# Longer rows and fewer transfers for the first stage's loads, with a new written order of that stage

## Chip, core and metric

The kernel runs on one core of a Trainium2 chip. The metric is the time of one execution on the device, in microseconds (us), median of three runs. Five engines work side by side: TensorE (PE, with its weight loads shown as PEld), VectorE (DVE), ScalarE (ACT), GpSimd (POOL) and SyncE (SP), which here only issues transfers. All transfers run on the core's 16 DMA engines.

## What is computed

One step of two transformer-like layers on 640 tokens (512 latent tokens and 128 prompt tokens) with 1024 channels. Cut to what the change touches, layer 0 begins so:

```
m     = silu(cond) @ w_mod[0] + b_mod[0]          # cond = c (latent) or c_ctx (prompt)
shift, scale = first two of the six 1024-wide parts of m
xm    = rmsnorm(x) * g * (1 + scale) + shift
q,k,v = split(xm @ w_qkv)                         # then attention, FFN, LRU layer, FFN
```

Everything is float32 in and out. Products that need precision are made of three products of rounded halves (hi*hi, hi*lo, lo*hi).

## The kernel before, in words

Activations lie transposed: channels on the 128 partitions in 8 blocks (index k), tokens along the row. The first stage, `start` (from line 339), makes shift and scale of the first sub-layer, the norm of x, the modulated x as two halves `hi` and `lo`, and the first eight blocks' sums of q and k of head pair 0. Behind it come attention (8 head pairs, up to about 350 us), the first FFN, the LRU layer and the second FFN, all of them chains of products on PE.

SP's queue of loads in the stage: the conditioning vectors (L1580), x in 8 transfers of one block each (L354, 320 KB, rows of 2560 bytes), then the adaLN weights `wm0` in 16 transfers of 512 KB with rows of 4 KB (`fetch`, L366): four groups g of two channel blocks, in each the scale part (j=1), then the shift part (j=0), each in two halves h of the contraction. Two weight tiles of q and k (L359) go behind the parts of group 0, two tiles of v behind all. SP issues a load when one of a few earlier ones has landed.

The stage's compute order on PE, DVE and ACT is written by hand in `START`, a list of steps that `in_order` chains on each engine. A letter is a step, the digits its arguments:

- `f`: a product of ones with 512 columns into a bank that nothing reads (L495), and `x`k n: the same with the first n columns of x block k (L492). Both only keep PE at work.
- `q`k, `a`k: square of x block k (ACT, L386) and its addition (DVE, L389). `m`: moments over the channels (PE, L394); `v j n`: variance, root and Newton step; `d`, `t`, `r`: diagonal matrix (DVE, L415), its spread over partitions (PE, L421), copy (ACT, L425).
- `p`g j h: a half piece of the adaLN product, 4 products of 256 columns (PE, L431; each has two instructions). `e`, `s`: copy and selection of a finished piece (ACT L436, PE L444). `A`k, `B`k: scale and shift of block k.
- `g`, `h`, `l`: x times scale and norm (DVE), its hi half (ACT), its lo half (DVE), for the latent (0) and prompt (1) tokens.
- `w`, `u`: hi and lo of a weight tile. `z`k part u: sums with block k, four products of 320 columns for part 0 (L481, L482) and two for part 1 (L479); `y`: the last eight (L488).

The order of work outside such lists is drawn up by a list scheduler at build time, from modelled times. The product that turns the conditioning vectors (L1582) stands ahead of the list in the program but is not in it; ScalarE's SiLU of them (L1583), the load of the table that holds the square root (L1585) and the copies that `p` needs hang on it. The first products of attention's v (L278) follow `y`.

Of the kernel before, what the change touches and what calls it, by code (L numbers as in the profile page):

```python
# [9 lines left out]
F32 = mybir.dt.float32  # L10
F32R = mybir.dt.float32r
AF = mybir.ActivationFunctionType
# [3 lines left out]
P = 128  # L16
D = 1024
KT = D // P
NLAT = 512
NTOK = 640  # L20
# [28 lines left out]
CHN = (3, 3, 4, 4, 4, 4)  # L49

START = (
# [6 lines left out]

TAIL = (
    "p0 T r0 p1 m r1 q0 q1 t1 p2 d r2 q2 t2 p3 x r3 s0 s1 q3 t3 p4 F0 r4 F2 s2 q4 t4 p5 r5 F4 s3 q5 t5 p6 r6 s4 F6 q6 s5 s6 p7 r7 q7 s7 y67 ")  # L60
# [6 lines left out]
def _lay(inp):  # L67
    g = {k: np.asarray(v) for k, v in inp.items()}

    def colmajor(v):  # L70
        return v.reshape(KT, P).T

    ng, cw = g["norm_g"], g["lru_conv_w"][0]
    vecs = [ng[0, 0], ng[0, 1], ng[1, 0], ng[1, 1], cw[0], cw[1], cw[2], cw[3], g["lru_conv_b"][0],
            g["lru_b_a"][0, 0], g["lru_b_a"][0, 1], g["lru_b_i"][0, 0], g["lru_b_i"][0, 1],
            g["lru_lam"][0, 0], g["lru_lam"][0, 1], g["state_h"][0, 0, 0], g["state_h"][0, 0, 1],
            g["b_mod"][0, :D], g["b_mod"][0, D:2 * D],
            g["final_g"], *(g["b_mod"][l, j * D:j * D + D] for l, j in MODS)]
    cols = np.concatenate([colmajor(v) for v in vecs], axis=1)

    rpb = g["attn_rpb"][0]

    def toeplitz(lo, hi, fill):
        e = np.full((NH, ROWS, 47, ROWS), fill, np.float32)
        for r in range(ROWS):
            e[:, r, lo + 23:hi + 24, :] = rpb[:, 7 - r:15 - r, lo + 15:hi + 16].transpose(0, 2, 1)
        return e

    inner = np.lib.stride_tricks.sliding_window_view(toeplitz(-15, 15, 0.0).reshape(NH, ROWS, 376), 256, axis=2)[:, :, 0:128:8]
    edge = np.stack([inner, inner], axis=1).transpose(0, 3, 2, 1, 4).reshape(NH, 16, ROWS, 2, 32, ROWS).copy()  # L90
    for i, c0 in enumerate((0, 48)):
        for cl in range(16):
            st = min(max(c0 + cl - 8, 0), 48)
            for j in range(32):
                if not st <= c0 - 8 + j < st + 16:
                    edge[:, 15 - cl, :, i, j] = NEG
    def tiles(w):
        return w.reshape(-1, P, w.shape[1] // P, P).transpose(2, 1, 0, 3)

    wq, gu, dn, wm = g["attn_w_qkv"][0], g["ffn_w_gu"], g["ffn_w_down"], g["w_mod"]  # L100
    arr = {
        "x": np.concatenate([np.roll(g["x_sample"].reshape(ROWS, 64, D).transpose(1, 0, 2), 8, axis=0).reshape(NLAT, D),
                             g["x_prompt"].reshape(P, D)]).T,
        "cc": np.stack([g["c"].reshape(KT, P), g["c_ctx"].reshape(KT, P)]).reshape(2 * KT, P),
        "ck": g["cache_k"].reshape(PAST, D).T,
        "cv": g["cache_v"].reshape(2, P, KT, P).transpose(2, 1, 0, 3),
        "wm0": wm[0, :, :2 * D].reshape(2, 4, P, 2, 4, 256).transpose(3, 4, 0, 2, 1, 5),
        "wm": wm.reshape(2, D, 6, D).transpose(0, 2, 3, 1).reshape(12, KT, P, D)[2:],
        "wqk": tiles(wq[:, :2 * D]),
        "wv": wq[:, 2 * D:].reshape(2, 4, P, 4, VW).transpose(3, 0, 2, 1, 4),  # L110
        "wo": tiles(g["attn_w_o"][0]),
        "wi": tiles(g["lru_w_in"][0]),
        "wg": np.stack([g["lru_w_a"][0], g["lru_w_i"][0]]).transpose(2, 3, 0, 1, 4),
        "wlo": tiles(g["lru_w_out"][0]),
        "gu": np.stack([tiles(w) for w in gu]),
        "dn": np.stack([tiles(w) for w in dn]),
        "cols": cols,
        "edge": edge.reshape(NH, P, 2, 256),
        "emid": toeplitz(-8, 7, NEG),
    }  # L120
    return {k: np.ascontiguousarray(v) for k, v in arr.items()}
# [13 lines left out]
def _pieces(t0, t1):  # L135
    return [(s, max(a, t0), min(b, t1)) for s, a, b in ((0, 0, NLAT), (1, NLAT, NTOK)) if max(a, t0) < min(b, t1)]


class _Step:
# [198 lines left out]
    def start(self, hi, lo, sp, big):  # L338
        nc, x = self.nc, self.x
# [9 lines left out]
        n = NB * P  # L349
        ssq = self.t([P, NTOK], F32, "ssq", 1, sp)  # L350
        rsb = self.t([P, NTOK], F32, "rsb", 1, sp)
        dg = self.t([P, NT, P], F32, "dg", 1, sp)
        for k in range(KT):
            nc.sync.dma_start(x[:, k], self.i["x"][k * P:k * P + P])  # L354
        raws = []

        def load(src):
# [3 lines left out]
        parts = {}  # L361

        def fetch(g, j):
            for h in range(2):
                w = self.t([P, 4, n], F32, f"sw{g}{j}{h}", 1, sp)
                nc.sync.dma_start(w, self.i["wm0"][j, g, h])  # L366
                parts[g, j, h] = w

        for g in range(KT // NB):
            for j in (1, 0):  # L370
                fetch(g, j)
                if g == 0:
                    load(self.i["wqk"][KT - j * KT])
# [7 lines left out]
        C, sq, pm, rows, pt, AB, z = _pieces(0, NTOK), [ssq], {}, {}, {}, {}, {}  # L381

        def square(k):
            if k:
                sq.append(idle[:, 2048 + k % 4 * NTOK:2688 + k % 4 * NTOK])
            nc.scalar.activation(sq[k], x[:, k], AF.Square)  # L386

        def add(k):
            nc.vector.tensor_tensor(ssq, ssq, sq[k], ALU.add)  # L389
# [104 lines left out]
        def fill():  # L494
            nc.tensor.matmul(acc[1][1], self.ones, self.ones.unsqueeze(1).broadcast_to([P, 4, P]), start=True, stop=True)  # L495

        steps = dict(f=fill, j=half, n=newton, q=square, a=add, m=moment, v=var, d=diag, t=spread, r=root, p=piece, e=row, s=select, A=scale, B=shift, g=gain, h=high, l=low,
                     w=weight, u=rest, z=sums, y=final, x=warm)
        with self.in_order():
# [367 lines left out]
    def heads_out(self, p, b0, pts, ppt, V, cv, op, O):  # L867
# [18 lines left out]
        for out, v, w, start, stop in parts():  # L886
            with self.tc.issue_after(first) if first is not None else nullcontext():
                mm = nc.tensor.matmul(out, v, w, start=start, stop=stop)  # L888
            first = first if first is not None else mm.ins
# [63 lines left out]
    def opening(self, w, hi, lo, gk, key, xd, l):  # L953
# [89 lines left out]
        with self.in_order():  # L1043
# [26 lines left out]
            f += 1  # L1070
            ps = mm(f, 1, range(KH))
            start(st)
            mm(f, 1, range(KH, KT), ps)
            gain(0, 0)
# [110 lines left out]
    def sum_weights(self, q, first=False):  # L1185
        for run, after in zip(self.s_sums(q), (self.pw, self.next)):
            with self.tc.issue_after(after):
                run(False)
        with self.tc.issue_after(self.last) if first else nullcontext():
            for i in range(2):  # L1190
                self.s_split(q, i)
# [355 lines left out]

    def load_x(self, src):
        for k in range(0, KT, 2):
            self.nc.sync.dma_start(self.x[:, k:k + 2], src[k * P:k * P + 2 * P].rearrange("(k p) t -> p k t", p=P))  # L1550

    def run(self):
        nc, tc, i, o = self.nc, self.tc, self.i, self.o
# [21 lines left out]
        with ExitStack() as banks:  # L1575
            self.pp = banks.enter_context(tc.tile_pool(name="psattn", bufs=1, space=bass.MemoryType.PSUM))
            self.begin(dict(tp=2, sp=2, op=1, quota=24))
            with tc.tile_pool(name="start", bufs=1) as sp:
                ccr = self.t([2 * KT, P], F32, "ccr", 1, sp)
                nc.sync.dma_start(ccr, i["cc"])  # L1580
                pc = self.ps("tp")
                nc.tensor.transpose(pc[:, :2 * KT], ccr, self.ident[:2 * KT, :2 * KT])  # L1582
                nc.scalar.activation(self.cs, pc[:, :2 * KT], AF.Silu)  # L1583
                nc.scalar.activation(ccr, ccr, AF.Silu)
                nc.scalar.activation(self.t([P, 1], F32, "dum", 1)[0:2 * KT], ccr[:, 0:1], AF.Sqrt, scale=0.0)  # L1585
                cd = dram.tile([2 * KT, P], F32, tag="cd", name="cd")
                nc.scalar.dma_start(cd, ccr)
                self.x = self.big(F32)
                acc, us = self.start(xhi, xlo, sp, wbig)
            self.mods = self.modulations()  # L1590

# [88 lines left out]
```

## Time and profile before

| | |
|---|---|
| median of 3 runs | 1486.8 us (1486.11 to 1486.82) |
| the profiled execution's own time | 1489.09 us |
| its span, first to last instruction | 1487.2 us |
| mean granted TensorE clock | 0.996 |
| PE busy | 1471.7 us (99%) |
| PEld / DVE / ACT busy | 97% / 73% / 49% |
| moved by DMA | 255.35 MB, mean 172 GB/s |

Busy PE time is modelled and overlaps; a PE that shows as busy can still wait between products. The granted clock is 1.00 at 2.4 GHz and 0.50 at 1.2 GHz. DMA share is the mean busy share of the 16 DMA engines: full stretches show 1.02 to 1.06.

### The profile page before, as it was taken

The numbers are of one execution on the slowest core, as the hardware profiler recorded it, in microseconds if no ns is written. First come the engines' busy times: TensorE is split into PE (matmuls) and PEld (weight loads), VectorE is DVE, ScalarE is ACT, GpSimd is POOL, SyncE is SP. The second block draws the span as 40 slices with busy tenths as digits, with TensorE's granted clock in tenths as the row PEclk, the third lists the DMA queues.
The fourth block names the chain that finished last, engine by engine and source line by source line (L and its number), as shares of the span: only waits on it lengthen the run. The fifth ranks groups of instructions, "written<-read, shape, count | busy, mean of one in ns | idle before, by whom it ended". The sixth has DMA issues, their size and how long they took to land.

```text
span 1487.2 us, 26374 instructions
## 1 busy us (share of the span) xinstructions
PE 1471.7 (99%) x10377; PEld 1439.8 (97%) x10377; DVE 1079.6 (73%) x2054; ACT 729.3 (49%) x1345; POOL 248.1 (17%) x325
## 2 busy tenths in 40 slices
PE   9999999999999999999999999999999999999997
PEld 5999999999999999999999999999999999999997
DVE  6788887876677788997876489985865665566555
ACT  5666766754333234323434298863644352434344
POOL 0001000000012222211210001112132322222311
PEclk9999999999999999999999999999999999999999
DMA  9545555443359899977863744267242231313122
GB/s 370 180 150 169 171 148 160 126 156 100 114 169 318 294 372 323 310 251 236 301 223 123 251 142 142 86 239 250 77 131 86 58 113 57 114 57 107 53 69 71
DMA packets 86026, 255.35 MB, mean 172 GB/s; under 512 B 9056, under 2 KB 22544, under 8 KB 85776
## 3 DMA queue, kind: packets, MB, share of 16 engines
q1 hardware_dynamic: 59152, 157.06, 32.4%
q0 software_dynamic: 26576, 96.49, 19.1%
q8 instruction: 81, 1.33, 0.4%
q14 instruction: 41, 0.34, 0.1%
q10 hardware_dynamic: 176, 0.13, 0.0%
HBM read 206.18 MB, written 43.53 MB: 168 GB/s over the span
## 4 chain that ended last, share of the span: by engine, by line
PE 89%; DVE 4%; DMA 3%; ACT 2%; issue 1%; POOL 1%; SPq 0%; DVEq 0%; ACTq 0%; POOLq 0%
PE mm L255 13%; PE mm L253 13%; PE mm L254 13%; PE mx L253 5%; PE mx L254 5%; PE mx L255 5%; PE mx L1203 3%; PE mx L1204 3%; PE mx L1205 3%; PE op L888 2%; PE gp L1412 2%; PE tp L806 2%; PE mc L1204 1%; PE mc L1203 1%; PE mc L1205 1%; PE mm L279 1%
## 5 line engine op out<-in xcount | busy, mean ns | idle before, releaser
L254 PE MATMUL mm<-big,whi 128*128 128x320 f32 (+3 forms) x1010 | 312.7, 310 | 0.3 <-DVE big L1530 0.3
L255 PE MATMUL mm<-big,wlo 128*128 128x320 f32 (+3 forms) x1010 | 312.2, 310 | 0.0
L253 PE MATMUL mm<-big,whi 128*128 128x320 f32 (+3 forms) x1010 | 310.9, 311 | 0.6 <-ACT big L1529 0.4
L292 DVE SCALAR_TENSOR_TENSOR mprod<-mraw,csb 128x1024 f32<-128x1024 f32 x160 | 195.0, 1218 | 18.2 <-DMA mraw<-in_wm 17.9
L254 PEld LDWEIGHTS mm<-big,whi 128*128 128x128 f32 x1010 | 190.5, 189 | 1.7 <-DVE big L1530 0.5
L253 PEld LDWEIGHTS mm<-big,whi 128*128 128x128 f32 x1010 | 189.6, 189 | 2.4 <-ACT big L1529 0.7
L255 PEld LDWEIGHTS mm<-big,wlo 128*128 128x128 f32 x1010 | 190.1, 189 | 1.0
L1529 ACT CAST whi<-raw 128x1024 fp32r<-128x1024 f32 (+2 forms) x103 | 105.4, 1025 | 150.9 <-PE mm L254 92.1
L1530 DVE TENSOR_TENSOR wlo<-raw,whi 128x1024 fp32r<-128x1024 f32 (+2 forms) x103 | 128.2, 1246 | 35.5 <-ACT whi L1529 35.3
L254 PE MATMUL mm<-big,whx 128*128 128x320 f32 (+3 forms) x443 | 137.4, 310 | 0.0
L255 PE MATMUL mm<-big,wlx 128*128 128x320 f32 (+3 forms) x443 | 137.3, 310 | 0.0
L253 PE MATMUL mm<-big,whx 128*128 128x320 f32 (+3 forms) x443 | 137.0, 310 | 0.0
L595 DVE SCALAR_TENSOR_TENSOR x<-mm,G,x 128x320 f32<-128x320 f32 (+3 forms) x202 | 81.4, 436 | 53.8 <-PE mm L255 48.5
L253 PE MATMUL mx<-big,whi 128*128 128x320 f32 (+3 forms) x318 | 99.3, 313 | 0.0
L254 PE MATMUL mx<-big,whi 128*128 128x320 f32 (+3 forms) x318 | 98.5, 310 | 0.1
L255 PE MATMUL mx<-big,wlo 128*128 128x320 f32 (+3 forms) x318 | 98.6, 310 | 0.0
L288 POOL DMA_DIRECT2D mraw<-in_wm x80 | 42.7, 534 | 311.5 <-DVE mprod L292 207.4
L254 PEld LDWEIGHTS mm<-big,whx 128*128 128x128 f32 x443 | 83.5, 189 | 0.0
L255 PEld LDWEIGHTS mm<-big,wlx 128*128 128x128 f32 x443 | 83.5, 189 | 0.0
L253 PEld LDWEIGHTS mm<-big,whx 128*128 128x128 f32 x443 | 83.4, 188 | 0.0
L1530 DVE TENSOR_TENSOR wlx<-sum,whx 128x1024 fp32r<-128x1024 f32 x40 | 51.0, 1274 | 35.1 <-ACT whx L1529 35.1
L255 PE MATMUL mx<-big,wlx 128*128 128x320 f32 (+3 forms) x229 | 70.9, 310 | 0.0
(396 smaller groups left out, 3854.4 us busy)
## 6 DMA issues: line engine op xcount, KB each, us to landing
raw<-in_gu SPq DMA_DIRECT2D x84, 512.0 KB, 3.7
mraw<-in_wm POOLq DMA_DIRECT2D x80, 512.0 KB, 5.4
raw<-in_dn SPq DMA_DIRECT2D x24, 512.0 KB, 3.6
sw<-in_wm SPq DMA_DIRECT2D x16, 512.0 KB, 10.1
raw<-in_wqk SPq DMA_DIRECT2D x16, 512.0 KB, 5.2
mraw<-in_wi POOLq DMA_DIRECT2D x16, 512.0 KB, 6.2
kwi<-kwh POOLq DMA_DIRECT2D x16, 512.0 KB, 6.0
kwi<-kwl POOLq DMA_DIRECT2D x16, 512.0 KB, 5.7
```

The source lines that it names most:

```text
L253: nc.tensor.matmul(ps, hi[:, k], xhi[:, k, s], start=(k == 0), stop=False)
L254: nc.tensor.matmul(ps, hi[:, k], xlo[:, k, s], start=False, stop=False)
L255: nc.tensor.matmul(ps, lo[:, k], xhi[:, k, s], start=False, stop=(k == nk - 1))
L288: nc.gpsimd.dma_start(w, self.i["wm"][l * 6 + j - 2, f])
L292: nc.vector.scalar_tensor_tensor(prod, w, 1.0, self.csb[:, s], ALU.mult, ALU.mult, accum_out=out[:, s, f:f + 1])
L595: last = self.nc.vector.scalar_tensor_tensor(xs, ps[:, a - t0:b - t0], G[:, s, f:f + 1], xs, ALU.mult, ALU.add).ins
L806: turn = nc.tensor.transpose(tp[:, j * P:j * P + P], s[:, j * P:j * P + P], self.ident)
L1203: nc.tensor.matmul(ps, hi[:, k], xh[:, k], start=start and k == 0, stop=False, skip_group_check=not start)
L1204: nc.tensor.matmul(ps, hi[:, k], xl[:, k], start=False, stop=False, skip_group_check=not start)
L1205: nc.tensor.matmul(ps, lo[:, k], xh[:, k], start=False, stop=(k == KH - 1), skip_group_check=not start)
L1529: high = self.nc.scalar.copy(hi, v).ins
L1530: return high, self.nc.vector.tensor_tensor(lo, v, hi.bitcast(F32), ALU.subtract).ins
```

## The change

x is laid out in memory so that two blocks of a partition follow each other (rows of 5120 bytes), loaded in four transfers of 640 KB; the tile that takes it is a view without gaps between blocks. The two halves of an adaLN piece become one transfer of 1 MB with rows of 8 KB, so both half pieces wait for the one transfer. The written order is new: three `f` at the head in place of one, other dummy products at other places, pieces and sums in another succession. The first square is placed behind the load of the square root's table. The second load of x, behind attention, takes the new layout too.

```diff
 START = (
-    "f x0288 x1288 x2288 x3288 x4288 x5288 x6288 x7288 q0 q1 a1 p010 q2 a2 q3 q4 a3 q5 q6 a4 q7 a5 a6 a7 m v p011 x6128 j n "
-    "e01 s01 p000 d0 A0 d1 x6128 t0 t1 w0 r0 A1 p001 x6256 x6256 r1 e00 w1 s00 B0 u0 g00 g11 x6128 p110 g01 g10 h01 l01 h00 "
-    "B1 h11 h10 p111 u1 z000 p100 z001 l11 p101 z100 l00 l10 e10 s10 z010 B3 z011 z110 A2 g20 A3 g21 z101 B2 p210 h20 g30 "
-    "p200 h21 p211 h30 g31 p201 h31 z201 e20 l21 s20 l20 p310 l31 z111 l30 A4 z200 B4 B5 g40 h40 p311 p300 A5 g41 g50 h41 "
-    "l41 g51 z210 h50 p301 h51 z211 z300 l40 e30 s30 z310 w2 l51 l50 z401 u2 z500 z411 w3 z400 A7 g71 B6 z510 z301 B7 A6 "
-    "h71 z501 g60 z311 l71 g61 z410 z511 g70 h60 h61 l61 z600 h70 l60 z601 z700 l70 z701 y ")
+    "f f f x0288 x1288 x2288 x3288 x4288 x5288 x6288 x7288 q0 q1 p010 q2 q3 q4 a1 a2 a3 a4 q5 q6 a5 a6 q7 a7 x7256 m v p011 x7128 j e01 p000 n s01 x6128 d0 "
+    "d1 t0 w0 A1 r0 t1 p001 A0 r1 x6256 x6128 e00 u0 g00 g01 s00 p110 g11 w1 p111 x6128 B0 h01 g10 B1 h00 p100 z000 h11 l01 u1 l11 h10 p101 l00 z001 e10 "
+    "l10 s10 z100 z011 A2 g20 z010 B2 z110 p210 A3 B3 g21 p200 g30 p211 g31 h20 h21 h30 l21 l20 p201 h31 z101 z201 l31 e20 s20 p310 z211 l30 B5 z111 A4 "
+    "z200 g40 p300 B4 h40 A5 g41 p311 h41 g50 l41 h50 p301 g51 h51 l40 e30 z210 z300 l51 l50 s30 z310 w2 z401 z500 z411 u2 A7 g71 B6 w3 z400 z510 B7 A6 g60 "
+    "h71 h60 z301 z501 l71 g61 g70 z311 z410 h61 z511 l61 z600 z601 h70 z701 z700 l60 l70 y ")
...
-                             g["x_prompt"].reshape(P, D)]).T,
+                             g["x_prompt"].reshape(P, D)]).T.reshape(4, 2, P, NTOK).transpose(0, 2, 1, 3),
...
-        "wm0": wm[0, :, :2 * D].reshape(2, 4, P, 2, 4, 256).transpose(3, 4, 0, 2, 1, 5),
+        "wm0": wm[0, :, :2 * D].reshape(KT, P, 2, 4, 256).transpose(2, 3, 1, 0, 4),
...
-        for k in range(KT):
-            nc.sync.dma_start(x[:, k], self.i["x"][k * P:k * P + P])
+        for k in range(0, KT, 2):
+            nc.sync.dma_start(x[:, k:k + 2], self.i["x"][k // 2])
...
         def fetch(g, j):
+            w = self.t([P, KT, n], F32, f"sw{g}{j}", 1, sp)
+            nc.sync.dma_start(w, self.i["wm0"][j, g])
             for h in range(2):
-                w = self.t([P, 4, n], F32, f"sw{g}{j}{h}", 1, sp)
-                nc.sync.dma_start(w, self.i["wm0"][j, g, h])
-                parts[g, j, h] = w
+                parts[g, j, h] = w[:, 4 * h:4 * h + 4]
...
-            nc.scalar.activation(sq[k], x[:, k], AF.Square)
+            with nullcontext() if k else self.tc.issue_after(self.table):
+                nc.scalar.activation(sq[k], x[:, k], AF.Square)
...
-            self.nc.sync.dma_start(self.x[:, k:k + 2], src[k * P:k * P + 2 * P].rearrange("(k p) t -> p k t", p=P))
+            self.nc.sync.dma_start(self.x[:, k:k + 2], src[k // 2] if len(src.shape) == 4 else src[k * P:k * P + 2 * P].rearrange("(k p) t -> p k t", p=P))
...
-                nc.scalar.activation(self.t([P, 1], F32, "dum", 1)[0:2 * KT], ccr[:, 0:1], AF.Sqrt, scale=0.0)
+                self.table = nc.scalar.activation(self.t([P, 1], F32, "dum", 1)[0:2 * KT], ccr[:, 0:1], AF.Sqrt, scale=0.0).ins
...
-                self.x = self.big(F32)
+                self.x = self.big(F32, NTOK + 2).rearrange("p k t -> p (k t)")[:, 0:KT * NTOK].rearrange("p (k t) -> p k t", k=KT)
```

## Rows read from the trace of the kernel before

**Rows 1.** Busy time by stretch: stretch, length, engines' busy us (instructions), clock, DMA share, GB/s.

```profile
0.00:50.00 50.00, 46.39 (x318) 32.61 (x319) 31.61 (x70) 28.41 (x60) 4.69 (x13) 0.93 0.85 316
50.00:100.00 50.00, 50.00 (x395) 48.33 (x395) 38.76 (x103) 34.27 (x70) 1.68 (x4) 1.00 0.57 175
```

**Rows 2.** The same view, the first stage cut where the granted clock changes.

```profile
8.00:14.70 6.70, 5.53 (x28) 2.81 (x28) 4.70 (x6) 3.68 (x5) 0.00 (x0) 0.98 1.03 414
14.70:21.60 6.90, 6.90 (x40) 4.88 (x44) 3.35 (x10) 2.08 (x5) 0.00 (x0) 0.52 1.03 416
21.60:24.80 3.20, 3.13 (x35) 1.92 (x27) 2.57 (x6) 2.84 (x8) 0.00 (x0) 1.00 1.03 410
24.80:36.50 11.70, 11.70 (x114) 7.84 (x114) 9.59 (x22) 6.29 (x17) 0.00 (x0) 1.00 1.02 408
36.50:47.00 10.50, 10.50 (x76) 9.85 (x75) 7.85 (x16) 5.72 (x14) 3.52 (x6) 1.00 0.43 131
```

**Rows 3.** The same view: rows of 2560 B (x), of 4 KB, of 8 KB (csb).

```profile
7.50:9.50 2.00, 1.48 (x5) 0.59 (x4) 1.49 (x3) 1.27 (x2) 0.00 (x0) 1.00 1.04 402
28.00:34.00 6.00, 6.00 (x66) 4.26 (x64) 4.67 (x12) 2.86 (x9) 0.00 (x0) 1.00 1.03 411
63.00:64.40 1.40, 1.40 (x10) 1.31 (x9) 1.18 (x5) 0.82 (x2) 0.00 (x0) 1.00 1.06 445
```

**Rows 4.** SP's timeline: adaLN loads p01 (second half last), p10's second half, p30's.

```profile
5.16 1.56 SPq L366 DMA_DIRECT2D sw<-in_wm  x2
...
13.98 0.33 SPq L366 DMA_DIRECT2D sw<-in_wm  x1
...
24.11 0.33 SPq L366 DMA_DIRECT2D sw<-in_wm  x1
```

**Rows 5.** DMA issues of these three windows: KB each, us from issue to landing.

```profile
sw<-in_wm SPq DMA_DIRECT2D x1, 512.0 KB, 7.5
...
sw<-in_wm SPq DMA_DIRECT2D x1, 512.0 KB, 10.1
...
sw<-in_wm SPq DMA_DIRECT2D x1, 512.0 KB, 11.6
```

**Rows 6.** The chain that ended last, first stage: start, us, what.

```profile
13.57 1.48 PE tp L394 x10
...
19.30 1.71 PE sp L421 x8
...
21.43 0.57 PE sp L431 x8
...
24.80 0.41 PE mm L481
```

**Rows 7.** PE's timeline, first stage: start, us, line, operation, columns, instructions.

```profile
1.09 2.08 PE L495 MATMUL op<-ones 128*128 128x512 f32 x2 [1.09 <-DVE ones L1562]
...
21.93 1.13 PE L492 MATMUL op<-big,ones 128*128 128x256 f32 x4
...
35.08 1.07 PE L431 MATMUL sp<-sw,csp 128*32 128x256 f32 x16
...
36.56 0.64 PE L431 MATMUL sp<-sw,csp 128*32 128x256 f32 x8
37.13 0.41 PE L479 MATMUL mm<-big,whi 128*128 128x320 f32 x1
...
46.95 0.39 PE L278 MATMUL mm<-whi,big 128*128 128x256 f32 x1
```

**Rows 8.** Timeline of PE, ACT and DVE: conditioning vectors, squares and their additions.

```profile
3.10 0.28 PE L1582 MATMUL tp<-ident,ccr 16*128 16x16 f32 x1
...
5.43 0.72 ACT L386 ACTIVATE ssq<-big 128x640 f32<-128x640 f32 x1
...
8.97 4.54 DVE L389 TENSOR_TENSOR ssq<-ssq,big 128x640 f32<-128x640 f32 x5 [0.40 <-ACT big L386]
```

## Prediction

> **What bounds the kernel now.** I read four views in this order: busy time by stretch, the chain that ended last, the timelines of the first stage, and the transfers. The stretches show a kernel that is held by PE [rows 1]: from 50 to 100 us the weight loads alone fill 48.33 of 50 us. Only the first 50 us differ: PE 46.39, weight loads 32.61, clock 0.93, DMA share 0.85. So the change can win only inside the first stage, and what it wins there stays won, because behind it the next products are always ready.
>
> Inside the stage three limits follow each other. Up to 13.5 us x arrives, is squared and added; the additions end at 8.97 + 4.54 = 13.51, and the moments start at 13.57 [rows 6, 8]. From there to 24.80, when the first sum of q runs, the norm passes through PE [rows 6]; from 14.70 to 21.60 the granted clock is 0.52, almost all of it at 1.2 GHz [rows 2]. From 24.80 on PE has a product in all of the time, at 1.00, until the first product of v at 46.95 [rows 2, 7]. Beside it the transfers run without a gap, 408 to 416 GB/s at a share of 1.02 or 1.03, up to about 36 us [rows 2]. The last adaLN load is issued at 24.11, takes 11.6 us and lands at 35.71 [rows 4, 5]; the piece that needs it, p301, runs at 36.56, hardly a microsecond later [rows 7]. PE and the transfers thus arrive there nearly together.
>
> **The parts of the change.** *Longer rows.* At a full share the rate by row length is 402 / 1.04 = 387 GB/s for 2560 bytes, 411 / 1.03 = 399 for 4 KB and 445 / 1.06 = 420 for 8 KB [rows 3]. For 5 KB I take 404, between the last two. x is 8 x 0.328 = 2.62 MB: 6.77 us become 6.49. The adaLN weights are 16 x 0.524 = 8.39 MB: 21.0 us become 20.0. Together 1.3 us at most. The row of 8 KB comes from a stretch of 1.4 us and from one source row read again and again, so it may flatter; the lower bound is 0. I take 1.0, nearer to the measured row. The last adaLN load then lands at 34.7 instead of 35.71.
>
> *Fewer, larger transfers.* A half piece now waits for the whole megabyte. For p010 the second half of old counts: issued at 5.16 + 1.56 - 0.33 = 6.39, landed 7.5 us later at 13.9 [rows 4, 5], some 0.4 us earlier by the longer rows, 13.5. In the new order PE comes to p010 and x7256 before the moments: 0.57 us for a half piece [rows 6] and about 0.5 us for 256 columns (1.13 us for two with the last one's end [rows 7]) put the moments at 14.6, 1.1 us later than before, although the additions would allow 13.6. This is the price of coarse loads, and it isn't hidden: v, j, n, d and the spread hang on it. SP issues 12 transfers fewer; it stood in no path, so that is worth nothing by itself, and were its cover gone it would cost the 0.33 us of an issue [rows 4].
>
> *The end of the pieces.* p300, p311 and p301 now follow each other, and p300 waits for the same megabyte as p301: 34.7 + 3 x 0.57 = 36.4, against the end of p301 at 37.13 before [rows 6, 7]. Behind p301 both lists hold the same 62 products of 320 columns, one selection and the ends, 46.95 - 37.13 = 9.82 us. So by the transfers alone the stage can end 0.7 us earlier and no more.
>
> *The same by PE.* Between z000 and the end of p301 the old list takes 37.13 - 24.80 = 12.33 us [rows 6, 7]. The new one has the same steps there, but p100 stands ahead of z000 (0.57 us less) and the list turns from sums to pieces five times where it was seven; such a turn is below 0.2 us, so 11.4 to 11.8. From the moments to the end of the spread took 21.43 - 13.57 = 7.86 us, from there to z000 3.37 [rows 6]. Of the 7.86 some 6.7 ran at half the clock, so the work is 1.1 + 3.4 = 4.5 us at full clock. *If the clock stays up*, the spread ends at 14.6 + 4.5 = 19.1, some tenths later for the serial steps of the norm; z000 could start at 23, but p100 ahead of it needs a megabyte whose second half landed at 13.98 + 10.1 = 24.1 [rows 4, 5], now about 23.5, and runs 0.57: z000 at 24.1, p301 done by 35.9. The transfers (36.4) then decide: 0.7 us gained. *If the clock falls as before*, 14.6 to 21.6 holds 3.5 us of the work, the last 1.0 follows: 22.6, z000 at 26.0, p301 done at 37.6, 0.5 us lost.
>
> *The dummy products.* Each f takes about 2 us at the head of the program, where 512 columns take 2.08 us although 256 later take half of about 1.0 [rows 7]: that is 1.2 GHz, whatever the mean of a stretch without a record would say. Two more cost nothing where PE waits for x anyway. But the product of the conditioning vectors at 3.10 could come to stand behind them, and with it the table load and the first square, 2.33 us after it [rows 8]; that is a rival below. The square's new place behind the table load is what the trace shows already, 0.
>
> *Elsewhere.* The second load of x and the tile without gaps stand beside 99% of PE work: 0.
>
> The sum: between 0.7 gained and 0.5 lost in the stage; I take 0.6 gained, since p300 and the clock both lean that way. The profiled execution took 1489.09 us, span 1487.2, 2.3 above the median of 1486.8; the difference is the same for both kernels, so I count from the median: **1486.2**.
>
> The Trainium skill, DMA: Bandwidth & Descriptors, section Rules for kernel authors, asks for at least 1 MiB per DMA for full bandwidth, and its section Bandwidth fits 2.0 us plus bytes / 436e3 per DMA. By an estimate from that page sixteen loads of 512 KB one by one take 51 us and eight of 1 MB 35. The rows do not bear it out: loads of 512 KB in a queue already run at 411 GB/s [rows 3].
>
> **The rivals.** (1) *The clock stays down, and the moments come late* (slower). The three f run ahead of the conditioning product, at 1.2 GHz: 3.10 + 2 x 1.8 = 6.7 [rows 7, 8]. The first square starts at 9.0, the additions some 1.4 us later and then 7 x 0.91 (4.54 / 5) = 6.4: 16.8. It decides once the additions end behind 14.6, so once the first square starts later than 6.8. With the clock down as before, the spread ends near 23.2, z000 at 26.6, p301 at 38.4: 1.3 us lost, 1488.1; without the late moments 0.5 lost, 1487.3. For it: the order of that product is the scheduler's, and one f stands ahead of it now. Against: it is earlier in the program and ready at about 3 us. (2) *The transfers gain more than the row length says*, as the rule would have it. As a mechanism here: the last megabyte lands before 34.2, PE alone decides, p301 ends at 35.9: 1.2 gained, 1485.6. (3) *The order behind the stage moves.* The scheduler draws it up anew from modelled times. From 50 to 100 us PE spends 1.7 us without loading weights [rows 1]; over the 300 us of attention that is 10 us at this rate, and a third of it either way is 3: 1483.5 or 1489.5. Nothing in the rows says which. (4) *The change does nothing*: rows of 8 KB bring 0, the pieces land as before at 35.7, p301 ends at 37.4: 0.3 lost, 1487.1.
>
> **How the numbers follow.** Forecast 0.40; rival 1 0.24, a third of it with late moments; rival 2 0.08; rival 3 0.18, half each way; rival 4 0.10. A measurement can tell about 0.2%, 3.0 us, from no change. Only rival 3 reaches beyond it, and misjudged sizes a little: faster 0.11, slower 0.09, same 0.80. The range leaves out the outer parts of rival 3 and takes in rivals 1, 2 and 4 with their bounds: 1483.9 to 1488.9.
>
> **What the profile of the changed kernel would show.** Right: a rate of 415 to 425 GB/s from 14 to 34 us; the moments at 14.6 behind p010; p300, p311 and p301 in one run that starts at 34.7 and waits for its load; the first product of v near 46.3. The clock is seen in a stretch from 14.7 to 21.6. Wrong: a first square after 6.8 us, a rate of 411, a stage that ends after 47.5, or a stretch behind 50 us whose products take another time than in the kernel before.

## The result, and the profile after

The changed kernel takes 1494.49 us (median of 7 runs, 1490.29 to 1499.39) against 1486.72 (1485.93 to 1488.44) for the kernel before on the same chips: ratio 1.0050, 95% interval 1.0033 to 1.0067. It is slower by 7.8 us, outside the predicted range. The profiled execution took 1495.46 us, span 1493.7, so 6.5 us more span than before. And 6.5 us is what the first stage lost: the first product of v stands at 53.43 in place of 46.95 [rows 7]. Behind it nothing was won or lost that this execution shows.

Busy time by stretch of the changed kernel, cut as in [rows 2] (stretch, length, busy us of PE, PEld, DVE, ACT and POOL with instructions, clock, DMA share, GB/s):

```profile
8.00:14.70 6.70, 4.21 (x20) 1.84 (x19) 3.75 (x5) 5.20 (x9) 0.00 (x0) 1.00 1.02 426
14.70:21.60 6.90, 4.60 (x28) 3.11 (x28) 3.78 (x10) 1.45 (x3) 0.00 (x0) 0.53 1.02 427
21.60:24.80 3.20, 3.20 (x19) 2.84 (x14) 1.60 (x3) 0.08 (x1) 0.00 (x0) 0.50 1.01 428
24.80:36.50 11.70, 11.70 (x81) 7.53 (x84) 6.52 (x14) 5.29 (x14) 0.00 (x0) 0.69 0.91 377
36.50:47.00 10.50, 10.50 (x109) 8.20 (x110) 8.96 (x19) 6.61 (x16) 0.00 (x0) 1.00 0.01 3
```

Two things stand out against [rows 2]. The transfers run faster (426 to 428 GB/s where it was 410 to 416) and are done by about 36 us: the last adaLN load is issued at 16.52, takes 17.0 us and lands at 33.5, while the pieces that need it run only at 42.04, so PE sets the end of the stage here and not the transfers. And the clock, low from 14.7 to 21.6 before, is now low up to about 32: the fourth stretch has a mean of 0.69, so 0.62 x 11.7 = 7.3 us of it are at 1.2 GHz.

The chain that ended last, first stage of the changed kernel (start, us, what):

```profile
2.13 6.60 DMA big<-in_x
8.75 0.34 ACTq L1587
9.13 0.74 ACT ssq L386
...
16.11 0.84 DVE ssq L389
17.00 2.29 PE tp L394 x10
...
23.62 1.71 PE sp L421 x8
...
32.42 0.35 PE mm L481
...
42.04 1.43 PE sp L431 x24
...
53.52 0.29 PE mm L277
```

The first square starts at 9.13 (before: 5.43 [rows 8]), the moments at 17.00 (13.57 [rows 6]), the first sum at 32.42 (24.80). From the moments to the first sum are 15.4 us where it was 11.2. What made the square late, and what PE did in the meantime, is in PE's timeline (start, us, line, operation, columns, instructions, and in brackets the idle time before it and what ended it):

```profile
1.09 4.68 PE L495 MATMUL op<-ones 128*128 128x512 f32 x6 [1.09 <-DVE ones L1562]
5.70 0.23 PE L1582 MATMUL tp<-ident,ccr 16*128 16x16 f32 x1
...
12.96 0.64 PE L431 MATMUL sp<-sw,csp 128*32 128x256 f32 x8 [1.36 <-DMA sw<-in_wm]
13.53 0.70 PE L492 MATMUL op<-big,ones 128*128 128x256 f32 x2
17.00 2.29 PE L394 MATMUL tp<-ones,ssq 128*128 128x1 f32 x10 [2.77 <-DVE ssq L389]
...
53.43 0.39 PE L277 MATMUL mm<-whi,big 128*128 128x256 f32 x1
```

All three f run ahead of the product of the conditioning vectors, which starts at 5.70 in place of 3.10. ACT's SiLU and table load follow it. Then ACT stands 0.7 us more, from 8.07 to 8.75, at the issue of the store L1587, which the chain puts down to a load of x. Then come the squares, and the additions run without a pause from 10.53 for 6.41 us:

```profile
10.53 6.41 DVE L389 TENSOR_TENSOR ssq<-ssq,big 128x640 f32<-128x640 f32 x7 [7.18 <-ACT big L386]
```

From 14.2 to 17.0 PE has no product, and about 15 us the clock falls.

### The profile page after: what moved, and what is told of

It reads as the page before. It is cut to its first block, busy times and chain, and to the rows that moved or that the text cites. A ratio compares the mean times of both kernels' runs of the same rounds, so it can differ in the third digit from the quotient of the medians.

```text
span 1493.7 us, 26370 instructions
## 1 busy us (share of the span) xinstructions
PE 1475.4 (99%) x10383; PEld 1443.1 (97%) x10383; DVE 1075.5 (72%) x2054; ACT 728.7 (49%) x1345; POOL 248.1 (17%) x325
## 4 chain that ended last, share of the span: by engine, by line
PE 88%; DMA 4%; DVE 4%; ACT 3%; issue 1%; POOL 1%; DVEq 0%; SPq 0%; ACTq 0%; POOLq 0%
PE mm L252 13%; PE mm L254 13%; PE mm L253 13%; PE mx L252 5%; PE mx L253 5%; PE mx L254 5%; PE mx L1203 3%; PE mx L1204 3%; PE mx L1205 3%; PE op L888 2%; PE gp L1412 2%; PE tp L806 2%; PE mc L1204 1%; PE mc L1203 1%; PE mc L1205 1%; PE mm L278 1%
```

## The experiments

Three theories were put up. **A**: the extra f delay the conditioning product, so table load, squares and moments; PE runs dry in front of the moments, and the clock falls and stays low. **B**: the coarse loads and the new succession cost by themselves. **C**: three f raise the clock early, and it falls back early for that reason.

### One f in place of three

```diff
-    "f f f x0288 x1288 ...
+    "f x0288 x1288 ...
```

> The changed kernel with one f at the head of the written order in place of three, all else as changed. Theory A (the two extra f delay the product of the conditioning vectors, so the table load, the squares and the moments, 17.00 us in the changed kernel; PE has no product from 14.2 to 17.0, and the granted clock falls and stays low for long): first square at 5.4 to 5.7, moments at 13.6 to 14.8, low clock for at most 7 us, first product of v at 46 to 47.6, time 1485.5 to 1488. Rival B (the coarse loads and the new succession cost by themselves, whatever the moments do): first product of v at 50 or later, time over 1490. Rival C (three f raise the clock early, and it falls back early for that reason, wherever they stand): as theory A here.

Measured: 1485.72 us (12 runs), ratio to the kernel before 0.9991 (0.9983 to 1.0000). Conditioning product 3.09, first square 5.43, moments 13.61, z000 22.91, first product of v 45.11. The clock does not fall any more. All of it is theory A's or a little better, and rival B is out: the same loads and the same succession are there.

The stage is now held by the transfers. Stretches of this run, then its half pieces late in the stage (PE's timeline), then the issue of the last three adaLN loads (SP's timeline) and the time to landing of the last (DMA issues, KB each):

```profile
14.70:21.60 6.90, 6.55 (x68) 4.34 (x68) 5.56 (x16) 4.47 (x11) 0.00 (x0) 1.00 1.01 425
...
24.80:36.50 11.70, 10.71 (x112) 7.91 (x110) 8.63 (x20) 6.39 (x15) 0.00 (x0) 1.00 0.92 378
```

```profile
28.58 1.50 PE L431 MATMUL sp<-sw,csp 128*32 128x256 f32 x24 [0.99 <-DMA sw<-in_wm]
...
33.68 1.50 PE L431 MATMUL sp<-sw,csp 128*32 128x256 f32 x24
...
45.11 0.38 PE L277 MATMUL mm<-whi,big 128*128 128x256 f32 x1
```

```profile
12.39 1.54 SPq L364 DMA_DIRECT2D sw<-in_wm  x3
```

```profile
sw<-in_wm SPq DMA_DIRECT2D x1, 1024.0 KB, 19.9
```

The last is issued at 12.39 + 1.54 - 0.33 = 13.60 and lands at 33.5; p300, p311 and p301 run as one block from 33.68, and v starts 11.4 us behind it. PE, busy throughout this stretch before, now shows 1 us of idle time in it, in front of pieces. The run below with the f behind the conditioning product has the same two blocks at 28.56 and 33.68, though its moments come 0.17 us later: the loads set these times.

### Three f, but behind the conditioning product

```diff
-                nc.tensor.transpose(pc[:, :2 * KT], ccr, self.ident[:2 * KT, :2 * KT])
+                self.turn = nc.tensor.transpose(pc[:, :2 * KT], ccr, self.ident[:2 * KT, :2 * KT]).ins
...
-            nc.tensor.matmul(acc[1][1], self.ones, ...
+            with self.tc.issue_after(self.turn):
+                nc.tensor.matmul(acc[1][1], self.ones, ...
```

> The changed kernel with its three f, but placed behind the product of the conditioning vectors. Theory A: that product at about 3.1, first square at 5.4 to 5.7, moments at 13.6 to 14.8, first product of v at 45.5 to 47.6, time 1484.5 to 1488. Rival B: v at 50 or later, over 1490. Rival C: the clock rises near 5 us as in the changed kernel and falls near 15 for over 10 us, v at 49 or later, time over 1489.

Measured: 1486.20 us, ratio 0.9996 (0.9987 to 1.0004), first product of v at 45.10. PE's timeline:

```profile
2.70 0.25 PE L1583 MATMUL tp<-ident,ccr 16*128 16x16 f32 x1 [2.70 <-DMA ccr<-in_cc]
2.88 5.07 PE L496 MATMUL op<-ones 128*128 128x512 f32 x6
...
13.78 1.17 PE L394 MATMUL tp<-ones,ssq 128*128 128x1 f32 x10
```

Rival C is out: the three f are there, and the clock stays at 1.00 from 8 us to the end of the stage. For three f it is the place that costs, not the number.

### The first square not held behind the table load

```diff
-            with nullcontext() if k else self.tc.issue_after(self.table):
-                nc.scalar.activation(sq[k], x[:, k], AF.Square)
+            nc.scalar.activation(sq[k], x[:, k], AF.Square)
```

> The changed kernel without the placing of the first square behind the table load: two squares go ahead of the conditioning work on ACT, six stay behind it. Theory A: the additions end at 15 to 16 in place of 16.94, moments at 15.2 to 16.2, so the gap on PE is about half as long, 1.0 to 2.0 us; time between those of the changed kernel and of the kernel before, 1487 to 1493. Rivals B and C: within 1 us of the changed kernel's median, 1493.5 to 1495.5.

Measured: 1488.93 us, ratio 1.0013 (1.0004 to 1.0022). Two squares run at 5.06 and 5.70, the others from 8.79 on; moments at 15.07 behind a gap of 1.23 us; v at 47.63. As theory A had it, half the gap and a smaller part of the loss. So the placing of the square costs where the table load is late; by itself, with one f, it costs nothing.

### The old loads with the new order

```diff
-        for k in range(0, KT, 2):
-            nc.sync.dma_start(x[:, k:k + 2], self.i["x"][k // 2])
+        for k in range(KT):
+            nc.sync.dma_start(x[:, k], self.i["x"][k * P:k * P + P])
...
-            w = self.t([P, KT, n], F32, f"sw{g}{j}", 1, sp)
-            nc.sync.dma_start(w, self.i["wm0"][j, g])
+                w = self.t([P, 4, n], F32, f"sw{g}{j}{h}", 1, sp)
+                nc.sync.dma_start(w, self.i["wm0"][j, g, h])
```

> The kernel before with the new written order (three f, first square behind the table load), but its own loads: x in eight transfers with rows of 2560 bytes, adaLN pieces in sixteen of 512 KB. Theory A: first square at 8 to 9.2, moments at 16 to 17.2, low clock for over 10 us from about 15, time 1490 to 1497 as with the new loads. Rival B, if the coarse loads are its part that counts: moments before 15, time 1486 to 1488.5.

Measured: 1491.27 us, ratio 1.0036 (1.0024 to 1.0047), moments at 15.48. The square came at 7.64 and the moments earlier than theory A's numbers, v stands at 48.17, and the low clock was shorter than the 10 us I had written down; the time is as expected, and B's alternative is missed by nearly 3 us. The moments in PE's timeline, and the stretch in which the clock is low (a mean of 0.84 over 21 us, so 6.7 us at 1.2 GHz):

```profile
15.48 1.28 PE L394 MATMUL tp<-ones,ssq 128*128 128x1 f32 x10 [1.60 <-DVE ssq L389]
```

```profile
13.00:34.00 21.00, 19.40 (x163) 13.40 (x157) 14.77 (x32) 9.01 (x21) 0.00 (x0) 0.84 1.03 413
```

The loss comes with the order and does not need the new loads. Whether they add to it (1.0036 here, 1.0050 with them) stays open, since the intervals overlap; that it is the f in the order and not the rest of it, the run with one f has shown.

### Two f

```diff
-    "f f f x0288 x1288 ...
+    "f f x0288 x1288 ...
```

> The changed kernel with two f at the head in place of three. Theory A (it is the lateness of the moments, and it has a threshold): the product of the conditioning vectors at about 4.6, first square at 6.7 to 7.2, additions done at 14.4 to 15.0, so moments 0.3 to 0.9 behind x7256 and hardly a gap on PE; the clock does not fall, or for one stretch of 6.8 us; first product of v at 45 to 46.5, time 1485 to 1487.5. Rival (each f costs in proportion): half of the changed kernel's loss, 1489 to 1491.

Measured: 1488.96 us, ratio 1.0015 (1.0005 to 1.0025), v at 47.59. My time was missed, and the rival's half of the loss by 0.04 us; as ratios, half of the changed kernel's loss would be 1.0025, the end of the interval, so the rival is not excluded. PE's timeline says why my time was missed:

```profile
4.80 0.28 PE L1582 MATMUL tp<-ident,ccr 16*128 16x16 f32 x1
...
13.01 0.70 PE L492 MATMUL op<-big,ones 128*128 128x256 f32 x2
14.97 1.28 PE L394 MATMUL tp<-ones,ssq 128*128 128x1 f32 x10 [1.26 <-DVE ssq L389]
```

The moments came where expected, but p010 and x7256 were done by 13.7, earlier than I had reckoned, so the gap was 1.26 us, and behind it the clock was low for 6.7 us. There is no free lateness as large as I thought. One of the eleven executions took 1485.84 us, though, at a mean clock of 0.999; the other ten show 0.995 to 0.997 and took 1488.10 or more.

### The gap filled

```diff
-a7 x7256 m v
+a7 x7256 x7288 x7288 x7288 x7288 x7288 x7288 m v
```

> The changed kernel, three f and late squares as they are, with six more dummy products of 288 columns (x7288) between x7256 and the moments, some 2.9 us at 2.4 GHz, where PE had none from 14.2 to 17.0. Theory A1 (the late moments cost mainly through the clock, which falls in the gap): moments still at 16.9 to 17.6, granted clock 1.00 from about 5 on without a fall; from the moments to z000 9.3 us as in the run with one f, then 11.6 and 9.8: first product of v at 47.2 to 48.6, time 1487 to 1489. Theory A2 (the late moments themselves cost, the clock is a companion): v at 50 or later, time over 1491.

This is the run that decides. It adds work to PE and changes nothing else. Measured: 1487.80 us (1487.13 to 1489.80), ratio 1.0007 (0.9998 to 1.0015). PE's timeline:

```profile
5.95 0.23 PE L1582 MATMUL tp<-ident,ccr 16*128 16x16 f32 x1
...
16.68 1.27 PE L394 MATMUL tp<-ones,ssq 128*128 128x1 f32 x10
...
25.17 0.41 PE L481 MATMUL mm<-big,whi 128*128 128x320 f32 x1
...
46.18 0.38 PE L277 MATMUL mm<-whi,big 128*128 128x256 f32 x1
```

The moments are as late as in the changed kernel (16.68 and 17.00), yet v starts at 46.18, not 53.43. Six useless products are worth 0.43% (1.0050 - 1.0007), 6.4 us. What the lateness costs without the clock is the rest, 1.0007 - 0.9991 against the run with one f: 0.16%, 2.4 us (at the first product of v it is 1.1 us). So theory A1 holds: late moments cost mainly through the clock. The moments came 0.2 us ahead of my range and v a full microsecond, since from the moments to z000 it was 8.5 us and not 9.3, and from there to v 21.0 and not 21.4.

### The store of the conditioning vectors on another queue

```diff
-                nc.scalar.dma_start(cd, ccr)
+                nc.gpsimd.dma_start(cd, ccr)
```

> The changed kernel with the store of the SiLU of the conditioning vectors (L1587) issued by GpSimd in place of ACT, where it stands ahead of the first square and waits until 8.75. Theory A: first square at 8.0 to 8.3 in place of 9.13, additions done at 15.7 to 16.1, moments at 15.8 to 16.3, the gap on PE 1.6 to 2.2 us; the low clock is shorter, 6.8 to 13 us; time 1488 to 1492. Rival (that wait is beside the path): 1493.5 to 1495.5.

Measured: 1490.87 us, ratio 1.0024 (1.0015 to 1.0033). From the conditioning product to the first square are 8.84 - 6.51 = 2.33 us in place of 9.13 - 5.70 = 3.43, so the wait at the store was worth 1.1 us. But the product itself came 0.8 us later in this execution (the three f took 5.49 us, not 4.68), the square at 8.84 and the moments at 16.68 behind a gap of 2.73 us, all outside my ranges. The time is inside. The products of the f by themselves, least, median and most ns of one, in the changed kernel and in this one:

```profile
L495 PE MATMUL op<-ones x6: 593/1061/1222, 1.1 to 5.2; 128*128 128x512 f32 x6
```

```profile
L495 PE MATMUL op<-ones x6: 1057/1057/1219, 1.1 to 5.5; 128*128 128x512 f32 x6
```

In the changed kernel the last of the six takes 593 ns, about half of the median; here all six are of the long kind. How long the f take thus depends on when the clock first rises, and that differed between the two executions: with three f at the head the six products took from 4.34 us (old loads) to 5.49 (here). This is read from the products, since the clock column shows 1.00 for all of these first microseconds.

### The new loads with the old order

```diff
 START = (
-    "f f f x0288 x1288 x2288 x3288 x4288 x5288 x6288 x7288 q0 q1 p010 q2 q3 q4 a1 a2 a3 a4 ...
+    "f x0288 x1288 x2288 x3288 x4288 x5288 x6288 x7288 q0 q1 a1 p010 q2 a2 q3 q4 a3 ...
```

> The new loads with the written order of before (one f), first square placed behind the table load. Theory A, in which the transfers set the stage's end where nothing is late: the last adaLN load lands near 33.5 as in the runs with one f, p301 done by 36 to 37, first product of v at 45.1 to 46.9, time 1485.3 to 1487.2. Rival (the new order is what gains with one f): v at 46.5 to 47.5, time 1486.3 to 1487.5, no better than before.

Measured: 1486.74 us, ratio 0.9998 (0.9989 to 1.0007), moments 13.27, z000 21.77, v at 44.96, 0.14 us ahead of theory A's range. The time lies in both ranges; v decides, which the rival had at 46.5 or later. The stage ends as early as with the new order and one f. Whether the new order gains anything beyond the loads (0.9991 against 0.9998, intervals that overlap) stays open; the profiles say no.

### The clock over all runs

The same stretch, 13 to 34 us, of nine kernels; the clock column gives the low time, 2 x (1 - clock) x 21 us. In order: before, changed, one f, f behind the conditioning product, square free, two f, gap filled, store on another queue, new loads with the old order:

```profile
13.00:34.00 21.00, 20.82 (x177) 14.19 (x169) 13.55 (x32) 9.25 (x22) 0.00 (x0) 0.84 1.03 413
```

```profile
13.00:34.00 21.00, 18.23 (x110) 11.57 (x111) 11.89 (x24) 7.34 (x17) 0.00 (x0) 0.59 1.01 424
```

```profile
13.00:34.00 21.00, 19.25 (x190) 13.56 (x190) 14.74 (x35) 10.12 (x25) 0.00 (x0) 1.00 1.01 423
```

```profile
13.00:34.00 21.00, 19.44 (x194) 13.58 (x190) 14.76 (x35) 10.14 (x25) 0.00 (x0) 1.00 1.01 423
```

```profile
13.00:34.00 21.00, 19.77 (x165) 13.76 (x161) 14.51 (x32) 8.92 (x21) 0.00 (x0) 0.84 1.01 424
```

```profile
13.00:34.00 21.00, 19.74 (x165) 13.87 (x162) 14.41 (x32) 8.94 (x21) 0.00 (x0) 0.84 1.01 423
```

```profile
13.00:34.00 21.00, 21.00 (x194) 15.07 (x187) 16.70 (x35) 10.37 (x25) 0.00 (x0) 1.00 1.01 423
```

```profile
13.00:34.00 21.00, 18.27 (x130) 12.62 (x126) 13.20 (x28) 7.79 (x19) 0.00 (x0) 0.76 1.01 424
```

```profile
13.00:34.00 21.00, 20.02 (x197) 13.19 (x190) 15.54 (x38) 11.16 (x26) 0.00 (x0) 1.00 1.01 423
```

Low for 6.7, 17.2, 0, 0, 6.7, 6.7, 0, 10.1 and 0 us. In the five kernels in which PE waited in front of the moments (1.23 to 2.77 us; the run with the old loads is the fifth), the clock fell in the profiled execution; in the four with the new loads in which it did not wait there, it stayed. The PE column hides this: 18.23 of 21 us busy at the worst, because work at the low clock keeps PE busy for longer (the spread L421, eight products, 1.91 us in the changed kernel and 1.06 with one f).

Two rows keep this from being a rule: a gap was neither needed for the fall nor always enough. In the kernel before, the clock fell near 14.5 us, while the moments ran, and in front of them stood a gap of only 0.1 us [rows 2]; and in the run with the gap filled, one of 1.42 us in front of p010 was not followed by a fall. PE's timeline of the one, then of the other:

```profile
12.82 0.64 PE L431 MATMUL sp<-sw,csp 128*32 128x256 f32 x8 [0.61 <-DMA sw<-in_wm]
13.57 1.48 PE L394 MATMUL tp<-ones,ssq 128*128 128x1 f32 x10
```

```profile
12.67 0.64 PE L431 MATMUL sp<-sw,csp 128*32 128x256 f32 x8 [1.42 <-DMA sw<-in_wm]
```

The mean granted clock of every execution is known, and the time goes with it. The changed kernel: three executions at 0.993 took 1494.58 to 1499.39 us, two at 0.995 took 1492.67 and 1494.49, two at 0.996 took 1490.29 and 1491.81. With the gap filled all eleven show 0.997 to 0.999. The profiled execution of the kernel before shows 0.996; of the 66 executions of that kernel measured beside the experiments only 3 do, and 46 show 0.998 or 0.999, as the runs whose traces have no fall. So the low stretch in [rows 2] is most likely not the usual case of the kernel before (this is its only trace), and v at 46.95 is late for it. The 1.8 to 2.0 us by which v comes earlier in the three kernels with no late moments (45.11, 45.10, 44.96) are therefore more than the loads are worth: the medians give 0.02 to 0.09%, 0.3 to 1.3 us, hardly beyond the noise.

## Why the prediction was wrong

**The step that failed** is the one on the dummy products: "Two more cost nothing where PE waits for x anyway." PE has no use for that time, but the order of the head is a queue: the conditioning product waits behind the f, and ACT behind that product. That they might stand there was the first rival, with 0.24 and a third of it for the late moments. The first square and the additions came out as it had them (9.0, measured 9.13; 16.8, measured 10.53 + 6.41 = 16.94), but the 9.0 is luck: it had the conditioning product at 6.7 and the square 2.33 us behind, and measured were 5.70, because the last of the f ran at the higher clock, and 3.43, because of the wait at the store. I held it less likely because the product is ready at about 3 us; but the trace has it behind all three f (presumably not ready yet by the times that the list scheduler reckons with, which no run looked at), and on the chip the first f alone lasted until 3 us. What the two added f cost, put at nothing, is 1.0050 - 0.9991 = 0.59%, 8.8 us.

**The price of that rival** was mis-sized too: 1.3 us against 7.8 (from 16.8 its own way of counting gives 23.7 for the end of the spread, not 23.2, and so 1.8). I let the clock fall and rise where it had in the kernel before, as if its place were given. It is not: here PE ran dry in front of the moments and the clock fell near 15 us, the work behind them ran at 1.2 GHz with waits in it, and the clock came back only at about 32 us, 17 us later. The first sum stands at 32.4, not at the 26.6 of the rival.

**The transfers** gained more than reckoned. The last load was to land at 34.7; in the run with one f it landed at 33.5, so 2.2 us earlier and not 1.0. One part I had not priced: from 2 to 8 us the queue of larger loads moves 361 GB/s where it was 314 (and 314 again in the run with the old loads and the new order). The kernel before, then the changed kernel:

```profile
2.00:8.00 6.00, 4.71 (x9) 1.80 (x7) 1.45 (x5) 4.63 (x11) 0.00 (x0) 1.00 0.98 314
```

```profile
2.00:8.00 6.00, 5.87 (x14) 2.77 (x13) 0.37 (x3) 2.68 (x8) 0.00 (x0) 1.00 0.98 361
```

That is 0.28 MB, 0.7 us at the later rate. Behind it 426 to 428 GB/s against 410 to 416 is 3%, some 0.75 us over 25 us. At a full share the 420 GB/s taken for rows of 8 KB was right (427 / 1.02 = 419); but the share stood at 1.02 where it had been 1.03, so 3% arrived and not 5%. What the other 0.7 us are was not taken apart. The Trainium skill, DMA: Bandwidth & Descriptors, section Rules for kernel authors, wants 1 MiB per DMA; the direction is right here, and the size in a full queue is these 3%, far from the factor that its fit for single loads would give. That fit stands in the page's section Anatomy of one DMA — SWDGE (gpsimd) path, not in Bandwidth as the prediction has it, and is for loads issued from GpSimd, while these are issued by SP.

**The coarse loads** cost nothing. The first megabyte lands at 12.8 in the changed kernel and at 12.4 with one f (p010 runs at 12.96 and 12.51), earlier than its second half did before (13.9), so the moments stand at 13.61 with one f and not at 14.6. Its load is issued at 3.27 where the first one was issued at 5.16 [rows 4], since four loads of x stand ahead of it and not eight:

```profile
3.27 0.43 SPq L364 DMA_DIRECT2D sw<-in_wm  x1
```

The prediction put the fewer issues at nothing. Whether they are also why the early rate is higher was not tested.

**What held**: with nothing late, the stage is bound by the last megabyte. p300, p311 and p301 in one block behind its landing, then 9.8 us of products: 33.5 + 1.7 + 9.8 = 45.0, measured 45.11. The forecast of 1486.2 is near what the change takes without its f in the wrong place, 1485.72 and 1486.20, but that is in part luck: the transfers gained twice what was reckoned, and the stage was counted from a trace with a low stretch that most executions of the kernel before do not seem to have. Likely for the same reason the 2.3 us between the profiled execution and the median were not "the same for both kernels": with one f the profiled execution took 1485.63, the median 1485.72. Rival 3, that the order behind the stage moves by itself, was not seen at its size of 3 us: from the first product of v to the end of the span are 1440.3 us before and after, and 1438.0 to 1439.3 in the eight experiments; a shift of 1 or 2 us could not be told from this scatter.

## What to carry to other kernels

A dummy product is not free because its engine is idle; ask what real instruction stands behind it in the queue, and who waits for that one. The first products of this program took 1.06 us for 512 columns and later ones 0.59, so a filler at the head is nearly twice as long as it looks in a warm stretch. Where a serial part of the norm leaves PE dry for a few microseconds, fillers right in front of the wait can pay: here six of them brought back 6.4 us. Not making the serial part late was worth more: the three f behind the conditioning product, or one f alone, brought back all of the loss. And look at the clock of several executions before you count from one trace: the one of the kernel before was not typical.

## What the runs showed of the hardware

In front of the moments a gap of 1.2 us without a product (two f, or the square free) and one of 1.60 (old loads) were followed by 6.7 us at 1.2 GHz, one of 2.77 us by 17.2, and one of 2.73 by 10.1. So the same gap doesn't always cost the same. The changed kernel's spread of 9 us, against 2.7 us with the gap filled, goes with the mean clock of its executions (0.993 to 0.996, against 0.997 to 0.999); why the clock stays low for longer in one execution than in another is open. The Trainium skill, TensorE: Matmul & The Clock Gate, Part 1: The HAM clock gate (the "warmup" mystery), says that the throttled clock is the default and activity releases it. The trace agrees: in the changed kernel the three f begin with products of 1.06 us or more and end with one of 0.59, and the filled gap kept 1.00.

An issue of a transfer can block compute: in the changed kernel the store L1587 stood ahead of the squares in ACT's queue and, by the chain, was held until a load of x, issued by SP, had landed at 8.73. Taking it off ACT shortened the way from the conditioning product to the first square by 1.1 us. It does not always block: with one f the same store was issued at 3.83, and the square came at 5.43, as before.
